# Gate and up products in Strassen's form, and FFNs over two halves of the tokens, in a one-core Hymba layer

## The chip, the core and the metric

The kernel runs on one core of a Trainium2 chip. Five engines work beside each other, each through its own list of instructions in order: TensorE (PE in the profile: matrix products and transposes into PSUM), VectorE (DVE), ScalarE (ACT), GpSimd (POOL) and SyncE (SP, which issues most of the DMAs). The metric is device time in microseconds (us) of one execution.

## The reference

One inference step of a layer over T = 1048 tokens: 16 meta tokens, 1024 of the prompt, 8 samples.

```python
h += 0.5 * swiglu(rmsnorm(h), ffn1_gate, ffn1_up, ffn1_down)
u  = rmsnorm(h) @ w_in              # 1024 -> 4*512 + 512 + 1024 + 8
#    HGRN2 heads (4, dim 128, chunked) and Mamba-2 heads (8, dim 64, chunked scan)
h += concat(hgrn_out, ssm_out) @ w_out
h += 0.5 * swiglu(rmsnorm(h), ffn2_gate, ffn2_up, ffn2_down)
y  = rmsnorm(h)                     # and the final states of both kinds of heads

def swiglu(x, wg, wu, wd):          # wg, wu: 1024 x 2816, wd: 2816 x 1024
    return (silu(x @ wg) * (x @ wu)) @ wd
```

All is float32. The two FFNs hold most of the arithmetic.

## The kernel before

The hidden state h lies feature-major: 8 tiles of 128 features x 1048 tokens. PE multiplies in a format of fewer bits (float32r), so every operand of a product of weights and activations is split into two such parts, x = hi + lo: ACT casts to hi, DVE subtracts hi from x to give lo. `mm3` (L125) makes one product of three matmuls: whi·xhi, whi·xlo, wlo·xhi (L127 to L129). `weights` (L101) reads a block of 128 x 1024 floats by one DMA on SP's queue into one of three `raw` buffers, casts it (L121, ACT) and subtracts (L122, DVE). The tokens are worked in three chunks of 384, 384 and 280 columns (CHUNKS), each in a PSUM bank; there are four banks of the pool `acc` and four of the pool `mis`.

An FFN (`ffn`, L261) goes over the 22 tiles f of 128 hidden features in groups of two. For each f, `gateup` makes x·gate and x·up for the three chunks: 2 x 3 x 8 x 3 = 144 matmuls. ACT takes the SiLU of the gate product (L279), DVE multiplies it with the up product (L283), and ACT and DVE split the result into hi and lo (L285, L286). After each group, `down` multiplies the group before it: 72 matmuls for each f, and 24 evictions by DVE, each adding half a PSUM bank to h (L316). The last `down` takes two groups, chunk by chunk, and calls `after` for every finished tile: `NormAfter` (L197) squares it (ACT, L173), adds the squares up (POOL, L174), sums over the features by a product with a matrix of ones (PE, L184), takes 1/sqrt by Ln and Exp (ACT, with a load of the table that holds both, L154) and makes the operands xhi and xlo of the next product (L190 to L192). Operands of a finished chunk are so made while PE works on the next chunk.

The start (`load_input`, L441) reads nine tiles of 128 tokens, normalizes them token-major, transposes them on PE (L460) into the operands xh and xl, and starts the FFN; after the first gate and up products, `residual` transposes the input a second time (L481) and copies it into h (L483). Between the FFNs come the input projection, the Mamba-2 scan, four HGRN2 heads and the output projection in two halves (`out_proj`, L1028), the second of which ends with `NormAfter` again. After the last `down` of the second FFN, `final` transposes h back, normalizes and writes the output.

No order is written out for the engines: the program issues operations in the order of the Python code, a scheduler gives each engine its list, fixed before the run, and semaphores hold an instruction at the head of its list until its inputs are there and its output buffer is free. What stands behind a waiting instruction on the same engine waits too.

Of the kernel before, what the change touches and what calls it, by code (L numbers as in the profile page):

```python
# [27 lines left out]
CHUNKS = [(0, 384), (384, 384), (768, 280)]  # L28
CW = 384
# [9 lines left out]
class Pack:  # L39
    """small tiles side by side in slots"""  # L40
# [22 lines left out]
class Core:  # L63
    def __init__(self, ctx, tc):
        self.nc = tc.nc
        self.tc = tc
        ent = ctx.enter_context
        self.const = ent(tc.tile_pool(name="const", bufs=1))
        self.wraw = ent(tc.tile_pool(name="wraw", bufs=3))
        self.wsp = ent(tc.tile_pool(name="wsp", bufs=3))  # L70
# [7 lines left out]
        self.finish_norm = None  # L78
# [8 lines left out]

    def t(self, w=CW, tag="t", bufs=7):
        t = self.tmp.tile([P, CW], F32, tag=tag, name=self.uid(tag), bufs=bufs)
        return t[:, :w]  # L90

# [9 lines left out]
    def weights(self, ap, tag=None):  # L101
        """loads [P, nk, nc_] of weights and splits them exactly into two float32r parts"""
        nc_ = ap.shape[-1]
        raw = self.wraw.tile([P, 1024], F32, tag="raw", name=self.uid("raw"))
# [9 lines left out]
        if tag is None:  # L114
            hi = self.wsp.tile([P, 1024], F32R, tag="whi", name=self.uid("whi"))
            lo = self.wsp.tile([P, 1024], F32R, tag="wlo", name=self.uid("wlo"))
        else:
            hi, lo = self.slot(tag, dt=F32R), self.slot(tag, dt=F32R)
        hv = hi[:, : nk * nc_].rearrange("p (k c) -> p k c", k=nk)
        lv = lo[:, : nk * nc_].rearrange("p (k c) -> p k c", k=nk)  # L120
# [4 lines left out]
    def mm3(self, ps, whi, wlo, xhi, xlo, first, last):  # L125
        mm = self.nc.tensor.matmul
        mm(ps, whi, xhi, start=first, stop=False)  # L127
        mm(ps, whi, xlo, start=False, stop=False)  # L128
        mm(ps, wlo, xhi, start=False, stop=last)  # L129
# [12 lines left out]
        # r = A / sqrt(v), then out = r * (3 A^2 - v r^2) with A^3 = 1/2  # L142
# [7 lines left out]
def rstd_wide(K, v, r, after):  # L150
    """r = 1 / sqrt(v), with one Newton step; v is overwritten"""
# [14 lines left out]
def norm_square(K, h, k, c, sq):  # L166
    c0, w = CHUNKS[c]
    nc = K.nc
    hs = h[k][:, c0 : c0 + w]
    if k == 0:  # L170
        return nc.scalar.activation(sq[:, :w], hs, AF.Square)
    t = K.t(w)
    r = nc.scalar.activation(t, hs, AF.Square)  # L173
    nc.gpsimd.tensor_add(sq[:, :w], sq[:, :w], t)  # L174
    return r


def norm_finish(K, h, c, sq, wcol, after):
    """the operands x = rmsnorm(h) * w of chunk c, in two float32r parts"""
    c0, w = CHUNKS[c]  # L180
    cs = slice(c0, c0 + w)
    nc = K.nc
    ps = K.psm()
    nc.tensor.matmul(ps[:, :w], K.ones[D], sq[:, :w], start=True, stop=True)  # L184
    r = K.t(w)
    K.rstd(r, ps[:, :w], w, after)

    def one(k):
        xn = K.t(w)
        nc.vector.scalar_tensor_tensor(xn, h[k][:, cs], wcol[:, k : k + 1], r, ALU.mult, ALU.mult)  # L190
        nc.scalar.copy(K.xhi[k][:, cs], xn)
        (nc.gpsimd if k % 4 == 3 else nc.vector).tensor_sub(K.xlo[k][:, cs], xn, K.xhi[k][:, cs].bitcast(F32))  # L192

    return [lambda k=k: one(k) for k in range(KT)]


class NormAfter:  # L197
    """the norm of h, chunk by chunk as h is finished; the operands of a chunk follow between the steps of the next one"""

    def __init__(self, K, h, wcol, spill=None):  # L200
        self.K, self.h, self.wcol, self.spill = K, h, wcol, spill
        self.sq = new_sq(K)
        self.todo = []

    def __call__(self, k, c):
        K = self.K
        an = norm_square(K, self.h, k, c, self.sq[c])
        if c == 2 and self.spill is not None:
            K.nc.sync.dma_start(self.spill[k * P : (k + 1) * P, :], self.h[k])
        if k == 2 and c > 0:  # L210
            self.finish(c - 1)
        for _ in range(2 if k >= 3 else 0):
            if self.todo:
                self.todo.pop(0)()
        if k == KT - 1:
            self.an = an
            if c == 2:
                K.finish_norm = lambda: self.finish(2)

    def finish(self, c):  # L220
        if c == 0:
            new_x(self.K)
        self.todo += norm_finish(self.K, self.h, c, self.sq[c], self.wcol, self.an)
        if c == 2:
            while self.todo:
                self.todo.pop(0)()


def new_x(K):
    K.xh, K.xl = (K.big.tile([P, KT, T], F32R, tag=n, name=K.uid(n), bufs=1) for n in ("xh", "xl"))  # L230
    K.xhi = [K.xh[:, k] for k in range(KT)]
    K.xlo = [K.xl[:, k] for k in range(KT)]


def new_sq(K):
    return [K.t(tag="sq", bufs=3) for c in range(3)]


def proj(K, wh, wl, evac, chunks=(0, 1, 2)):
    """evac(c0, w, ps) for each chunk of tokens of x @ w"""  # L240
# [8 lines left out]
def proj_first(K, units):  # L249
    """the units after a norm: the last chunk of tokens is ready later than the others"""  # L250
    for c in (0, 1):
        for i, (wh, wl, evac) in enumerate(units):
            proj(K, wh, wl, evac, (c,))
            if K.finish_norm is not None and i == 1:
                K.finish_norm()
                K.finish_norm = None
    for wh, wl, evac in units:
        proj(K, wh, wl, evac, (2,))


def ffn(K, h, wg, wu, wd, after, ready=None, start=None):  # L261
    nc = K.nc
    NG = DFF // 256
    wgv = wg.rearrange("(k p) c -> p k c", p=P)
    wuv = wu.rearrange("(k p) c -> p k c", p=P)
    wdv = wd.rearrange("(g j p) c -> g p j c", p=P, j=2)

    def gateup(g):
        hh, hl = [], []
        for j in range(2):  # L270
            hh.append(K.slot("u", dt=F32R))
            hl.append(K.slot("u", dt=F32R))
        for j in range(2):
            fs = slice((2 * g + j) * P, (2 * g + j + 1) * P)
            ss = {}

            def ev_g(c0, w, ps):
                ss[c0] = K.t(w)
                nc.scalar.activation(ss[c0], ps, AF.Silu)  # L279

            def ev_u(c0, w, ps):
                hd = ss[c0]
                nc.vector.tensor_mul(hd, ps, hd)  # L283
                hiv = hh[j][:, c0 : c0 + w]
                nc.scalar.copy(hiv, hd)  # L285
                nc.vector.tensor_sub(hl[j][:, c0 : c0 + w], hd, hiv.bitcast(F32))  # L286

            if ready is not None and g == 0 and j == 0:
                ws = ready
            else:  # L290
                ws = [K.weights(wgv[:, :, fs]), K.weights(wuv[:, :, fs])]
            units = [(*ws[0], ev_g), (*ws[1], ev_u)]
            if g == 0 and j == 0:
                proj_first(K, units)
                if start is not None:
                    start()
            else:
                for un in units:
                    proj(K, *un)
        return hh, hl  # L300

    def down(gs, hids, chunk_major):
        sp = [[K.weights(wdv[g, :, :, q * 512 : (q + 1) * 512], "u" if len(gs) == 2 and q == 1 else None) for q in range(2)] for g in gs]

        def one(o, c):
            c0, w = CHUNKS[c]
            f = (o % 4) * P
            ps = K.psum()
            n = len(gs) * 2
            for i in range(n):  # L310
                dh, dl = sp[i // 2][o // 4]
                hh, hl = hids[i // 2]
                j = i % 2
                K.mm3(ps[:, :w], dh[:, j, f : f + P], dl[:, j, f : f + P], hh[j][:, c0 : c0 + w], hl[j][:, c0 : c0 + w], i == 0, i == n - 1)
            hs = h[o][:, c0 : c0 + w]
            nc.vector.scalar_tensor_tensor(hs, ps[:, :w], 0.5, hs, ALU.mult, ALU.add)  # L316

        if not chunk_major:
            for o in range(KT):
                for c in range(3):  # L320
                    one(o, c)
        else:
            for c in range(3):
                for o in range(KT):
# [868 lines left out]
```

## Time and profile before

| what | value |
|---|---|
| median of 3 runs | 2220.14 us (2210.18 to 2220.63) |
| the profiled execution: span, and its granted TensorE clock | 2218.1 us, 0.988 |
| busy: PE, DVE, ACT, POOL | 2155.6, 992.8, 597.3, 141.5 us |
| instructions: PE, DVE, ACT | 13770, 1824, 1065 |
| DMA queue of the loads and stores | 127.48 MB, 18.5% of 16 engines |
| first FFN, steady part (66 to 780 us): PE, DVE, ACT busy | 714.0, 255.6, 130.0 us of 714 |
| middle (820 to 1390 us): PE, DVE, ACT busy | 549.5, 336.5, 235.0 us of 570 |
| second FFN, steady part (1450 to 2190 us): PE, DVE, ACT busy | 740.0, 273.1, 133.9 us of 740 |

Busy time is the sum of an engine's instructions, as a share of the span or of a stretch of it. A matmul's recorded time is longer than the distance to the next one, since matmuls are pipelined; the distance between starts is what a matmul costs in a full stream. The profiled execution has no time of its own beside its span; it lies 0.1% under the median.

### The profile page before, as it was taken

What the parts mean: (1) busy time and instruction counts of PE and PEld (TensorE: products, weight loads), DVE (VectorE), ACT (ScalarE), POOL (GpSimd) and SP (SyncE); (2) the same over time, 40 slices, a digit from 0 to 9 for tenths busy, and PEclk for the clock granted to TensorE, in tenths of its full rate; (3) what the DMA queues carried; (4) which work ended last, traced back from release to release, by engine and by line L of the source; (5) the groups of instructions that cost most, each with busy time, mean ns of one, the idle gap of its engine ahead of it and who ended that gap; (6) DMA issues with size and microseconds to landing.
All of it is one profiled execution on the core that took longest, in us unless ns stands there. A gap on an engine that the chain in (4) does not pass through costs nothing.

```text
span 2218.1 us, 32029 instructions
## 1 busy us (share of the span) xinstructions
PE 2155.6 (97%) x13770; PEld 2111.5 (95%) x13770; DVE 992.8 (45%) x1824; ACT 597.3 (27%) x1065; POOL 141.5 (6%) x173
## 2 busy tenths in 40 slices
PE   6999999999999999989999999999999999999998
PEld 5999999999999989968989999999999999999997
DVE  6333334333343376577445466634334343343425
ACT  5311111111111243473522433431111111111112
POOL 1000000000000130231001000400000000000000
PEclk9999999999999999989999999999999999999999
DMA  4111111111111121162212142111111111111112
GB/s 146 48 48 48 44 42 48 48 48 48 40 47 48 58 100 45 55 196 61 82 50 65 55 144 72 29 39 48 48 48 40 47 48 48 48 48 39 48 39 77
DMA packets 173734, 132.19 MB, mean 60 GB/s; under 512 B 8664, under 2 KB 154320, under 8 KB 173584
## 3 DMA queue, kind: packets, MB, share of 16 engines
q1 hardware_dynamic: 172648, 127.48, 18.5%
q10 hardware_dynamic: 720, 2.62, 0.3%
q8 instruction: 108, 1.77, 0.3%
q14 instruction: 34, 0.28, 0.0%
q0 software_dynamic: 224, 0.04, 0.0%
HBM read 114.62 MB, written 15.56 MB: 59 GB/s over the span
## 4 chain that ended last, share of the span: by engine, by line
PE 87%; DVE 5%; issue 3%; DMA 2%; ACT 1%; POOL 1%; SPq 0%; DVEq 0%; POOLq 0%; ACTq 0%
PE acc L128 27%; PE acc L129 27%; PE acc L127 27%; PE mis L923 1%; DVE t L190 1%; DVE xl L192 0%; DMA raw<-in_w_ffn_up_dram 0%; DMA s<-cumd 0%; PE mis L1019 0%; PE mis L481 0%; DMA sst<-sbd 0%; PE mis L962 0%; PE mis L1067 0%; PE mis L980 0%; PE mis L692 0%
## 5 line engine op out<-in xcount | busy, mean ns | idle before, releaser
L127 PE MATMUL acc<-xh,whi 128*128 128x384 f32 (+1 forms) x2880 | 932.7, 324 | 2.2 <-ACT whi L121 1.5
L128 PE MATMUL acc<-xl,whi 128*128 128x384 f32 (+1 forms) x2880 | 933.0, 324 | 0.7 <-DVE xl L464 0.6
L129 PE MATMUL acc<-xh,wlo 128*128 128x384 f32 (+1 forms) x2880 | 931.1, 323 | 0.0
L127 PEld LDWEIGHTS acc<-xh,whi 128*128 128x128 f32 x2880 | 543.0, 189 | 4.2 <-ACT whi L121 1.7
L128 PEld LDWEIGHTS acc<-xl,whi 128*128 128x128 f32 x2880 | 543.4, 189 | 2.6 <-DVE xl L464 1.3
L129 PEld LDWEIGHTS acc<-xh,wlo 128*128 128x128 f32 x2880 | 543.3, 189 | 0.9
L122 DVE TENSOR_TENSOR wlo<-raw,whi 128x1024 fp32r<-128x1024 f32 x162 | 199.3, 1231 | 532.7 <-ACT whi L121 532.0
L121 ACT CAST whi<-raw 128x1024 fp32r<-128x1024 f32 x162 | 169.9, 1049 | 638.1 <-PE acc L128 443.0
L127 PE MATMUL acc<-u,whi 128*128 128x384 f32 (+1 forms) x1008 | 327.6, 325 | 0.0
L128 PE MATMUL acc<-u,whi 128*128 128x384 f32 (+1 forms) x1008 | 326.0, 323 | 0.0
L129 PE MATMUL acc<-u,wlo 128*128 128x384 f32 (+1 forms) x1008 | 325.4, 323 | 0.0
L316 DVE SCALAR_TENSOR_TENSOR s<-acc,s 128x384 f32<-128x384 f32 (+1 forms) x480 | 242.9, 519 | 169.2 <-PE acc L129 167.9
L127 PEld LDWEIGHTS acc<-u,whi 128*128 128x128 f32 x1008 | 190.3, 189 | 0.9 <-issue 0.6
L128 PEld LDWEIGHTS acc<-u,whi 128*128 128x128 f32 x1008 | 190.2, 189 | 0.9 <-issue 0.6
L129 PEld LDWEIGHTS acc<-u,wlo 128*128 128x128 f32 x1008 | 190.2, 189 | 0.0
L283 DVE TENSOR_TENSOR t<-acc,t 128x384 f32<-128x384 f32 x132 | 68.8, 521 | 247.8 <-PE acc L129 245.2
L285 ACT CAST u<-t 128x384 fp32r<-128x384 f32 x132 | 63.7, 483 | 305.1 <-DVE t L283 305.1
L279 ACT ACTIVATE t<-acc 128x384 f32<-128x384 f32 x132 | 60.8, 461 | 281.6 <-PE acc L129 281.5
L174 POOL TENSOR_TENSOR sq<-sq,t 128x384 f32<-128x384 f32 (+1 forms) x42 | 43.3, 1032 | 848.0 <-ACT t L173 796.5
L286 DVE TENSOR_TENSOR u<-t,u 128x384 fp32r<-128x384 f32 x132 | 68.6, 520 | 51.7 <-ACT u L285 51.6
L923 PEld LDWEIGHTS mis<-s,u 128*128 128x128 f32 x320 | 39.0, 197 | 7.9 <-issue 7.8
L129 PE MATMUL acc<-u,u 128*128 128x384 f32 (+1 forms) x144 | 46.4, 322 | 0.0
(326 smaller groups left out, 1454.8 us busy)
## 6 DMA issues: line engine op xcount, KB each, us to landing
raw<-in_w_ffn_gate_dram SPq DMA_DIRECT2D x44, 512.0 KB
raw<-in_w_ffn_up_dram SPq DMA_DIRECT2D x44, 512.0 KB
raw<-in_w_ffn_down_dram SPq DMA_DIRECT2D x44, 512.0 KB
raw<-in_w_in_dram SPq DMA_DIRECT2D x28, 512.0 KB
hspill<-s SPq DMA_DIRECT2D x8, 524.0 KB
s<-hspill SPq DMA_DIRECT2D x8, 524.0 KB
s<-cumd SPq DMA_DIRECT2D x8, 512.0 KB
raw<-in_w_out_dram SPq DMA_DIRECT2D x16, 256.0 KB
```

The costliest lines, as they stand in the source:

```text
L121: self.nc.scalar.copy(hv, src)
L122: self.nc.vector.tensor_sub(lv, src, hv.bitcast(F32))
L127: mm(ps, whi, xhi, start=first, stop=False)
L128: mm(ps, whi, xlo, start=False, stop=False)
L129: mm(ps, wlo, xhi, start=False, stop=last)
L174: nc.gpsimd.tensor_add(sq[:, :w], sq[:, :w], t)
L279: nc.scalar.activation(ss[c0], ps, AF.Silu)
L283: nc.vector.tensor_mul(hd, ps, hd)
L285: nc.scalar.copy(hiv, hd)
L286: nc.vector.tensor_sub(hl[j][:, c0 : c0 + w], hd, hiv.bitcast(F32))
L316: nc.vector.scalar_tensor_tensor(hs, ps[:, :w], 0.5, hs, ALU.mult, ALU.add)
L923: nc.tensor.matmul(ps[:, 64 * c : 64 * c + 64], kg[:, P * c : P * (c + 1)], qv[:, c, :, 1], start=True, stop=True)
```

## The change

Write the gate weights of one tile f over the two halves of the 1024 input features as A11 and A12, the up weights as A21 and A22, and the operand over the same halves, for one half of the tokens (524) split into two quarters of 262, as B11, B12, B21, B22. Gate and up of both quarters are four sums of two block products, eight in all. Strassen's form (in Winograd's variant) makes them of seven block products of sums of blocks, and sums of their results.

In detail:

- `gateup` works one f for one half of the tokens: 7 products of 4 x 3 = 84 matmuls of 262 columns. The weights need four block sums (128 x 512, L289, DVE) and seven splits (128 x 512: cast L294 on ACT, subtraction L295 on DVE). The products go to four PSUM banks a, b, c, d (all of `acc`), three of which are used twice; the sums of results are five additions of 262 columns on DVE (L312, L315, L318, L322, L325), then the SiLUs (L320, L323, ACT), the product (524 columns, L326) and the split of the result (L329, L330).
- `strassen_x` makes the seven operands of one half of the tokens from the normalized h: 8 products with the norm (L229), 8 subtractions (L238), 14 casts (L246) and 14 subtractions of hi (L247), each 128 x 524.
- `ffn` goes over the two halves of the tokens and, in each, over all 22 f, so every gate, up and down weight is read and split twice. `down` takes groups of 2, 4, 4, 4, 4, 4 tiles f; its products are of 262 columns and go to the banks of `mis`; its weights are 4 units of 128 x 1024 for each group and half. After the 22nd f of the first half, `more()` makes the operands of the second half, ahead of the last `down` in the code; after the second half, `between()` makes the first operands of the next stage likewise.
- The norm is the class `Norm`, by quarters of 262 tokens; its 1/sqrt is kept for all tokens (R), and the operands are made from it.
- The input is transposed once: `place` transposes a raw tile into h and makes its norm factor as a row by a product of ones with a diagonal matrix. Five tiles are read and placed first; the other four after the first `gateup` (`later`).
- The second half of the output projection goes over the two halves of the tokens, its weights read and split twice; after the first, `strassen_x` is called for the second FFN. CHUNKS, used by the middle alone, become 350, 350 and 348. The `raw` pool has 4 buffers, and one pool of 6 buffers (`ws`) takes the place of whi and wlo.

```diff
-CHUNKS = [(0, 384), (384, 384), (768, 280)]
+Q = T // 4
+CHUNKS = [(0, 350), (350, 350), (700, 348)]
...
+def strassen_x(K, h, r, wcol, half):
+    nc = K.nc
+    cs = slice(2 * Q * half, 2 * Q * half + 2 * Q)
+    xn = []
+    for kp in range(4):
+        t = K.slot("u", w=4 * Q).rearrange("p (k n) -> p k n", k=2)
+        for j in range(2):
+            k = 2 * kp + j
+            nc.vector.scalar_tensor_tensor(t[:, j], h[k][:, cs], wcol[:, k : k + 1], r[:, cs], ALU.mult, ALU.mult)
+        xn.append(t)
...
+    def operand(x):
+        t = K.xo().rearrange("p s (k n) -> p s k n", k=4)
+        for p in range(2):
+            ks = slice(2 * p, 2 * p + 2)
+            nc.scalar.copy(t[:, 0, ks], x[p])
+            nc.vector.tensor_sub(t[:, 1, ks], x[p], t[:, 0, ks].bitcast(F32))
+        return t
+
+    ops = [operand(b11)]
+    t1 = minus(b12, b11)
+    t2 = minus(b22, t1)
+    ops += [operand(t2), operand(t1), operand(minus(b22, b12)), operand(b21), operand(b22), operand(minus(b21, t2))]
+    return ops
...
+def gateup(K, wg, wu, f, ops):
...
+    def product(ps, x, i, first=True):
+        w = split(x)
+        for k in range(4):
+            hi, lo = w[:, k * P : k * P + P], w[:, 512 + k * P : 512 + k * P + P]
+            K.mm3(ps, hi, lo, ops[i][:, 0, k], ops[i][:, 1, k], first and k == 0, k == 3, not first)
+
+    a, b, c, d = (K.psum()[:, :Q] for i in range(4))
+    product(a, a11, 0)
+    z = K.tq()
+    nc.scalar.copy(z, a)
+    s1 = sum_(a21, a22, ALU.add)
+    s2 = sum_(s1, a11, ALU.subtract)
+    product(b, s2, 1)
+    v = K.tq()
+    nc.vector.tensor_add(v, b, z)
+    product(c, s1, 2)
+    w5 = K.tq()
+    nc.vector.tensor_add(w5, c, v)
+    product(d, sum_(a11, a21, ALU.subtract), 3)
+    gt, ut = (K.t(2 * Q).rearrange("p (n t) -> p n t", n=2) for i in range(2))
+    nc.vector.tensor_add(ut[:, 1], d, w5)
+    product(a, a12, 4, False)
+    nc.scalar.activation(gt[:, 0], a, AF.Silu)
+    product(c, sum_(a12, s2, ALU.subtract), 5, False)
+    nc.vector.tensor_add(gt[:, 1], c, v)
+    nc.scalar.activation(gt[:, 1], gt[:, 1], AF.Silu)
+    product(d, a22, 6, False)
+    nc.vector.tensor_add(ut[:, 0], d, v)
+    nc.vector.tensor_mul(gt, gt, ut)
+    gt = gt.rearrange("p n t -> p (n t)")
+    hid = K.slot("u", w=4 * Q, dt=F32R).rearrange("p (s t) -> p s t", s=2)
+    nc.scalar.copy(hid[:, 0], gt)
+    nc.vector.tensor_sub(hid[:, 1], gt, hid[:, 0].bitcast(F32))
+    return hid
...
+    for half in range(2):
+        hids, f0, due = [], 0, []
+        for f in range(NF):
+            hids.append(gateup(K, wgv, wuv, f, ops))
+            if half == 0 and f == 0 and start is not None:
+                start()
+            if due:
+                down(half, *due.pop(), False)
+            if f % 4 == 1 and f < NF - 1:
+                due.append((f0, hids))
+                hids, f0 = [], f + 1
+        if half == 0:
+            ops = more()
+        else:
+            between()
+        down(half, f0, hids, True)
...
+    for i in range(5):
+        read(i)
+    parameters(K, a)
+    for i in range(5):
+        place(i)
+
+    def later():
+        for i in range(5, 9):
+            read(i)
+            place(i)
...
-    out_proj(K, a, h, 1, opb, NormAfter(K, h, K.pc["norm_ffn2"]))
+    def after2(k, q):
+        nf2.add(k, q)
+        if k == KT - 1 and q == 1:
+            ops.extend(strassen_x(K, h, nf2.r, wn2, 0))
```

More of the change, by code (lines that the diff above doesn't have):

```diff
@@ L113, in weights, with split @@
         src = raw[:, : nk * nc_].rearrange("p (k c) -> p k c", k=nk)
[L114 to L120, printed above, removed]
+        return self.split(src, self.ws(), self.ws())
+    def split(self, src, hi, lo):
+        n, k, c = src.shape
+        hv = hi[:, : k * c].rearrange("p (k c) -> p k c", k=k)
+        lv = lo[:, : k * c].rearrange("p (k c) -> p k c", k=k)
         self.nc.scalar.copy(hv, src)
@@ L197 @@
[L197 to L226, printed above, removed]
@@ L229, in new_x, with __init__, add @@
[L229 to L236, printed above, removed]
+class Norm:
+    def __init__(self, K, h):
+        self.K, self.h = K, h
+        self.r = K.big.tile([P, T], F32, tag="R", name=K.uid("R"), bufs=1)
+        self.sq = {}
+    def add(self, k, q):
+        K = self.K
+        hs = self.h[k][:, q * Q : q * Q + Q]
+        if k == 0:
+            self.sq[q] = K.t(Q)
+            an = K.nc.scalar.activation(self.sq[q], hs, AF.Square)
+        else:
+            t = K.t(Q)
+            an = K.nc.scalar.activation(t, hs, AF.Square)
+            K.nc.gpsimd.tensor_add(self.sq[q], self.sq[q], t)
+        if k == KT - 1:
+            ps = K.psm()
+            K.nc.tensor.matmul(ps[:, :Q], K.ones[D], self.sq[q], start=True, stop=True)
+            K.rstd(self.r[:, q * Q : q * Q + Q], ps[:, :Q], Q, an)
@@ L249, in proj_first, with sum_, split @@
 def proj_first(K, units):
-    for c in (0, 1):
-        for i, (wh, wl, evac) in enumerate(units):
+    for c in range(3):
+        for wh, wl, evac in units:
             proj(K, wh, wl, evac, (c,))
[L254 to L261, printed above, removed]
-    nc = K.nc
-    NG = DFF // 256
+def gateup(K, wg, wu, f, ops):
+    nc = K.nc
+    fs = slice(f * P, f * P + P)
+    raws = []
+    for w in (wg, wu):
+        t = K.raw()
+        nc.sync.dma_start(t.rearrange("p (k c) -> p k c", k=KT), w[:, :, fs])
+        raws.append(t)
+    a11, a12 = raws[0][:, 0:512], raws[0][:, 512:1024]
+    a21, a22 = raws[1][:, 0:512], raws[1][:, 512:1024]
+    def sum_(x, y, op):
+        t = K.t(512)
+        nc.vector.tensor_tensor(t, x, y, op)
+        return t
+    def split(x):
+        t = K.ws()
+        nc.scalar.copy(t[:, 0:512], x)
+        nc.vector.tensor_sub(t[:, 512:1024], x, t[:, 0:512].bitcast(F32))
+        return t
+    def product(ps, x, i, first=True):
[31 more added lines that the diff above has]
+    return hid
@@ L264, in ffn @@
+def ffn(K, h, wg, wu, wd, ops, more, between, after, start=None):
+    nc = K.nc
+    NF = DFF // P
     wgv = wg.rearrange("(k p) c -> p k c", p=P)
     wuv = wu.rearrange("(k p) c -> p k c", p=P)
[L266 to L321, printed above, removed]
-        else:
-            for c in range(3):
-                for o in range(KT):
-                    one(o, c)
-                    after(o, c)
@@ L328, in ffn, with down, unit, one @@
-    prev = None
-    for g in range(NG):
-        cur = gateup(g)
-        if g == NG - 1:
-            down([g - 1, g], [prev, cur], True)
-        elif prev is not None:
-            down([g - 1], [prev], False)
-        prev = cur
+    wdv = wd.rearrange("(f p) c -> p f c", p=P)
+    def down(half, f0, hids, last):
+        n = len(hids)
+        def unit(q, tag=None):
+            raw = K.raw()[:, : n * 256].rearrange("p (f c) -> p f c", f=n)
+            nc.sync.dma_start(raw, wdv[:, f0 : f0 + n, q * 256 : q * 256 + 256])
+            parts = [K.slot(tag, dt=F32R) if tag else K.ws() for i in range(2)]
+            return K.split(raw, *parts)
+        def one(un, o, c):
+            ps = K.psm()[:, :Q]
+            fs = slice((o % 2) * P, (o % 2) * P + P)
+            for i, hid in enumerate(hids):
+                K.mm3(ps, un[0][:, i, fs], un[1][:, i, fs], hid[:, 0, c * Q : c * Q + Q], hid[:, 1, c * Q : c * Q + Q], i == 0, i == n - 1)
+            q = 2 * half + c
+            hs = h[o][:, q * Q : q * Q + Q]
+            nc.vector.scalar_tensor_tensor(hs, ps, 0.5, hs, ALU.mult, ALU.add)
+            if last:
+                after(o, q)
+        if last and half == 1:
+            units = [unit(q, "u" if q >= 2 else None) for q in range(4)]
+            for c in range(2):
+                for o in range(KT):
+                    one(units[o // 2], o, c)
+        else:
+            for q in range(4):
+                un = unit(q)
+                for o in (2 * q, 2 * q + 1):
+                    for c in range(2):
+                        one(un, o, c)
@@ L753, in sample @@
     def sample(b):
-        s = K.wraw.tile([P, 1024], F32, tag="raw", name=K.uid("sst"))
+        s = K.raw("sst")
         sb = s[:, 0:512].rearrange("p (j n) -> p j n", j=4)
@@ L989, in samples @@
     def samples(b0):
-        s = K.wraw.tile([P, 1024], F32, tag="raw", name=K.uid("hst"))
+        s = K.raw("hst")
         sb = s[:, 0:512].rearrange("p (b v) -> p b v", b=4)
```

202 lines of the change are left out of this document (106 added, 96 removed).

## The prediction

> **What bounds the kernel now.** I read the page first (busy shares, the chain that ended last), then busy times by stretch, then the starts of matmuls in a full stream, the DVE groups by shape, and last the idle times of PE at the seams.
>
> ```profile
> span 2218.1 us, 32029 instructions
> ...
> PE 2155.6 (97%) x13770; PEld 2111.5 (95%) x13770; DVE 992.8 (45%) x1824; ACT 597.3 (27%) x1065; POOL 141.5 (6%) x173
> ...
> PE 87%; DVE 5%; issue 3%; DMA 2%; ACT 1%; POOL 1%; SPq 0%; DVEq 0%; POOLq 0%; ACTq 0%
> ```
> PE is the bound: 97% busy, 87% of the chain.
>
> ```profile
> 0.00:25.00 25.00, 5.08 (x24) 3.98 (x24) 11.40 (x34) 13.92 (x25) 10.16 (x34) 1.00 0.83 277
> 25.00:66.00 41.00, 39.79 (x264) 37.37 (x265) 31.09 (x92) 24.88 (x62) 0.00 (x0) 0.96 0.19 55
> 66.00:780.00 714.00, 714.00 (x4462) 713.23 (x4462) 255.58 (x427) 129.97 (x214) 8.09 (x8) 1.00 0.15 46
> 780.00:820.00 40.00, 35.59 (x220) 34.07 (x219) 30.50 (x49) 22.07 (x41) 18.16 (x20) 0.96 0.39 137
> ```
> Columns: stretch, then busy us of PE, PE's weight loads, DVE, ACT, POOL, granted clock, DMA share, GB/s. Inside the first FFN PE never stops and DVE works 36% of the time; PE's idle lies at the start and at the seams.
>
> ```profile
> 303.63 0.33 PE L129 MATMUL acc<-xh,wlo 128*128 128x384 f32 x1
> 303.80 0.29 PE L127 MATMUL acc<-xh,whi 128*128 128x280 f32 x1
> 303.93 0.29 PE L128 MATMUL acc<-xl,whi 128*128 128x280 f32 x1
> 304.06 0.29 PE L129 MATMUL acc<-xh,wlo 128*128 128x280 f32 x1
> ...
> 816.80 0.34 PE L129 MATMUL acc<-xh,wlo 128*128 128x384 f32 x1
> 818.23 0.74 PE L184 MATMUL mis<-sq,ones 128*128 128x280 f32 x2 [1.09 <-POOL sq L174]
> ```
> First column: start. A matmul costs the distance between starts: from 299.78 to 303.80 the 23 of 384 columns take 174.8 ns each, the 24 of 280 to 306.89 take 128.8. So time goes by columns (0.46 ns each). After the 1.4 us gap at 816.8 the stream goes on at full rate.
>
> ```profile
> L122 DVE TENSOR_TENSOR wlo<-raw,whi 128x1024 fp32r<-128x1024 f32 x162 | 199.3, 1231 | 532.7 <-ACT whi L121 532.0
> L316 DVE SCALAR_TENSOR_TENSOR s<-acc,s 128x384 f32<-128x384 f32 x320 | 174.7, 555 | 138.0 <-PE acc L129 136.7
> L286 DVE TENSOR_TENSOR u<-t,u 128x384 fp32r<-128x384 f32 x88 | 49.1, 558 | 51.2 <-ACT u L285 51.1
> ...
> L464 DVE TENSOR_TENSOR xl<-mis,xh 128x512 fp32r<-128x512 f32 x16 | 10.2, 682 | 1.5 <-ACT xh L463 1.5
> ```
> ```profile
> 31.73 1.29 DVE L464 TENSOR_TENSOR xl<-mis,xh 128x512 fp32r<-128x512 f32 x2 [0.83 <-ACT xh L463]
> ```
> DVE prices by width (mean ns behind the bar). Two of 512 back to back take 1.29 us, so one fills 0.61 and ends 0.68 after its start. By width I estimate 0.34 (0.42 to its end) for 262 columns, 0.62 for 524, 0.65 for 524 with the norm (half of the 1284 ns of L456), 1.14 for 1024 (1231 less the same 0.08).
>
> **The change, part by part.** The sum is against the profiled 2218.1 us, 0.1% under the median.
>
> *PE's columns.* Gate and up of one f: 48 matmuls on each chunk, 48 x (2 x 0.1748 + 0.1288) = 22.96 us. After: 2 x 84 = 168 of 262 columns. At 0.46 ns a column 0.1205 each, 20.24 us. Times 44: -120. Down: 24 x (2 x 0.1748 + 0.1288) = 11.48 to 96 x 0.1205 = 11.57 us, times 44: +4. Net **-116**. The 262-wide step isn't in the trace: its ends are 0.112 (the 16 transposes of L481 take 1.75 us, 0.109 each, so a weight load fits under that) and 0.1288 (no shorter than 280), -99 and +96 on 11,616 matmuls; I take 0.1205, as 262 is 6% from 280.
>
> *A new wait in each gateup.* The static order of after puts on DVE's queue, behind product d's end: the sum into ut (L318), the sum a12 - s2 for product 5 (L289), then two sums for the *next* f, and only then the subtraction of product 5 (L295). From the end of product d: 0.2 (hand-over, as L283 starts after L129) + 0.42 + 0.60 + 0.60 + 0.68 + 0.68 = 3.2 us until product 5 has its lo. PE has meanwhile product 4 (12 matmuls, 1.45) and the six of product 5 that need hi alone (0.72): 2.17. So PE stands about 1.0 us in 64 of 88 gateups; in the 24 ahead of a down no next sums stand there and ACT's cast ends last, about 0.8. **+84** (35 to 130: four DVE steps at 0.45, or at 0.75). Behind that subtraction the next f's splits queue, but those have 3 us of PE work as cover. DVE's whole need is 11 x 0.61 + 5 x 0.34 + 2 x 0.62 = 9.7 us for 10.12 us of PE: no slack to catch up. ACT's need (7 casts of 0.60 from L463's 588 ns, 4 smaller: about 6 us) hides under PE.
>
> *Loads.* FFN weights are read twice, about +70 MB on 127: the queue's 18.5% becomes about 29%. A pair of raw tiles has a gateup's 11 us to land where one takes 4.5: hidden, 0; without cover it would be 4.5 us a gateup.
>
> *Start.* Now the first real matmul starts at 25.1, the first f ends at 57.0 (22.96 us of it work) and the second transposes (L481) take 7.9: 42 us beside the work. After: 5 tiles are copied into h by DVE and ACT in turn till about 32 us; then on DVE 8 norm products (to 36), and 23 further operations ahead of product 1's lo, so product 0 starts near 37, product 1 near 51, the first gateup ends near 64. Then PE's list has the transposes of tiles 5 to 8 behind product 0 of the second gateup, and tile 5's load is on ACT's queue behind the first gateup's last cast: it lands near 71, and each tile has its chain of square (1.06 us), table load (1.28), 1/sqrt. The second gateup goes on near 88 to 94 with 11.6 us of work done: 65 to 82 beside the work. **+35** (+10 if SP and ACT issue the loads at once, +45).
>
> *Middle of FFN 1.* `more()` puts 28 to 30 operations of `strassen_x` (8 x 0.65 + 22 x 0.62 = 19 us) on DVE ahead of the down's first eviction (L359). PE has four banks of `mis`, 4 x 1.45 = 5.8 us after about 2 us of waiting for the hid; it stands about 12 to 15. At the next half's first gateup the Exp of `Norm` stands ahead of the casts on ACT: 7 to 8. With 2 for the clock **+23** (12 to 30).
>
> *FFN 1 to the middle.* `between()`: 16 operands and 4 unit splits, about 15 us of DVE, ahead of the first eviction: stands 10.5 where now 4.4 + 1.5 are lost: **+5** (-3 to +10).
>
> *Output projection to FFN 2.* Now 4.5 + 2.5 are lost. After: `strassen_x` (28 operations) ahead of an eviction while four `acc` banks hold 5.8 us: 13, and 8 for the norm at the end, 2 for the clock: **+16** (5 to 25).
>
> *Middle of FFN 2.* As in FFN 1, 15, and the `final` of tiles 0 to 3 on PE ahead of the next product 0, 5: **+20** (8 to 28).
>
> *Clock.* After the 3.3 us idle at 794 the 280-wide matmuls run at 0.233 from 798.7 to 801: half rate, 1.7 us lost. With four new long gaps **+6**. Chunks of 350 have the same columns: 0.
>
> Sum: -116 + 84 + 35 + 23 + 5 + 16 + 20 + 6 = +73: about **2290 us** (+3%).
>
> **Rivals.**
> 1. *DVE's queue is not on the path* (faster). Then the 84 and the DVE blocks (15 + 15 + 13 + 5 at the seams) are hidden: -132, **2158**. For it: DVE is 45% busy and waits now on PE or ACT in nearly every group. Against it: the order is fixed, the sums for the next f stand ahead. At half of that cost the time is 2224 (*same*, between 2207 and 2229); faster by over 0.5% from under 0.37 of it.
> 2. *DVE sets the pace of each gateup*: its operations wait for one another, so each costs its whole duration: 11 x 0.68 + 5 x 0.42 + 2 x 0.70 = 11.0 and the 0.8 of waiting for PE, 11.9 in place of 11.1 in 64 gateups: +50, **2340**. For it: no slack. Against: back-to-back pairs overlap (1.29 for two).
> 3. *The clock falls at every stall*: 1.7 us lost in each of 88 gateups, +150, **2440**. Against it: the 1.4 us gap at 816.8 left the rate alone. [...]
>
> **How the numbers follow.** Forecast 2255 to 2325: 0.52. Rival 2: 0.17. Rival 3: 0.04. Same: 0.09. Rival 1: 0.18. A change of 0.5% (11 us) is about what runs of this kernel can tell from none. Slower 0.73, same 0.09, faster 0.18. The range leaves out most of rival 1, rival 3 and the upper edge of 2: 2190 to 2345.
>
> **What would show it.** PE starts of 262 columns every 0.1205 us. One idle time of about 1 us on PE in each gateup, ahead of product 5, put down to DVE ws L295; PE share near 90%, DVE above 75%. PE idle of over 10 us three times, ahead of L359's evictions, and product 1 of the first gateup near 51 us. Wrong it is if DVE shows idle time ended by PE all through the gateups, or if the 262-wide step is not in proportion to its columns.

## The result

The changed kernel takes 2398.84 us (median of 4, 2396.52 to 2404.74) against 2216.57 us for the kernel before (4 runs): 1.0828 times as long, 95% interval 1.0798 to 1.0857. The forecast was 2290 us, slower, with a range from 2190 to 2345: the direction was right, the size was less than half of what came. The profiled execution took 2404.74 us, its span is 2403.0, so 185 us have to be found against the 2218.1 of before.

The page of the changed kernel, in the order in which the page of before was read (span, busy shares, the costliest PE, DVE and ACT groups of the gate and up products):

```profile
span 2403.0 us, 39323 instructions
...
PE 2147.0 (89%) x15928; PEld 2051.3 (85%) x15928; DVE 1646.1 (68%) x3121; ACT 933.6 (39%) x1782; POOL 133.7 (6%) x175
...
L140 PE MATMUL acc<-xo,ws 128*128 128x262 f32 (+2 forms) x3232 | 989.6, 306 | 122.1 <-ACT ws L294 68.9
...
L295 DVE TENSOR_TENSOR ws<-t,ws 128x512 fp32r<-128x512 f32 x352 | 239.9, 687 | 71.3 <-ACT ws L294 67.4
...
L294 ACT CAST ws<-t 128x512 fp32r<-128x512 f32 x352 | 208.0, 617 | 102.4 <-PE mis L141 79.7
```

PE's share fell from 97% to 89%; it stands idle for 256 us in place of 62. The prices of the operations are those of the prediction (a subtraction of 512 columns 0.687 us, a cast 0.617). DVE works 68% of the time, and it, too, has long idle times: it is not the bound by its sum.

Busy times by stretch (stretch, busy us of PE, its weight loads, DVE, ACT, POOL, granted clock, DMA share, GB/s): the start, the first half of FFN 1, its middle, its second half, the seam to the middle of the kernel, then the seam to FFN 2 and the middle of FFN 2:

```profile
0.00:88.20 88.20, 38.02 (x188) 34.04 (x188) 52.01 (x168) 38.99 (x96) 10.13 (x34) 0.73 0.28 86
88.20:445.50 357.30, 336.10 (x2615) 323.76 (x2616) 261.70 (x474) 133.74 (x252) 0.00 (x0) 0.99 0.30 88
445.50:495.40 49.90, 28.90 (x212) 27.61 (x210) 34.97 (x61) 22.77 (x44) 11.12 (x14) 0.79 0.18 51
495.40:863.90 368.50, 346.17 (x2699) 333.41 (x2700) 273.11 (x498) 138.33 (x264) 0.30 (x3) 1.00 0.30 88
863.90:910.60 46.70, 33.15 (x230) 31.28 (x229) 35.15 (x70) 24.45 (x48) 12.59 (x14) 0.83 0.56 175
...
1486.00:1558.40 72.40, 52.88 (x406) 51.24 (x404) 47.05 (x84) 36.94 (x68) 24.84 (x28) 0.90 0.15 44
...
1928.00:1983.80 55.80, 30.99 (x228) 29.75 (x226) 39.84 (x89) 17.82 (x40) 0.00 (x0) 0.78 0.16 54
```

Two kinds of loss show. PE is idle for 50 us at the start and for 14 to 25 at each of the four seams, where the clock is lower as well (0.73 to 0.90). And it is idle for 21 to 22 us in each half of an FFN, where before it never stopped.

What happens in the steady part is the same in each gateup. PE's matmuls around product 5 (first column: start):

```profile
298.52 0.28 PE L142 MATMUL acc<-xo,ws 128*128 128x262 f32 x1
299.79 0.39 PE L140 MATMUL acc<-xo,ws 128*128 128x262 f32 x1 [0.99 <-DVE t L289]
300.02 0.29 PE L141 MATMUL acc<-xo,ws 128*128 128x262 f32 x1
300.31 0.39 PE L140 MATMUL acc<-xo,ws 128*128 128x262 f32 x1
300.53 0.28 PE L141 MATMUL acc<-xo,ws 128*128 128x262 f32 x1
300.83 0.39 PE L140 MATMUL acc<-xo,ws 128*128 128x262 f32 x1
301.06 0.28 PE L141 MATMUL acc<-xo,ws 128*128 128x262 f32 x1
301.18 0.28 PE L142 MATMUL acc<-xo,ws 128*128 128x262 f32 x1
301.30 0.28 PE L140 MATMUL acc<-xo,ws 128*128 128x262 f32 x1
```

and ACT and DVE in the same time:

```profile
298.84 0.39 ACT L320 ACTIVATE t<-acc 128x262 f32<-128x262 f32 x1 [3.91 <-PE acc L142]
299.13 0.61 ACT L294 CAST ws<-t 128x512 fp32r<-128x512 f32 x1
...
299.63 1.14 ACT L294 CAST ws<-raw 128x512 fp32r<-128x512 f32 x2
```
```profile
297.38 0.43 DVE L318 TENSOR_TENSOR t<-acc,tq 128x262 f32<-128x262 f32 x1 [0.88 <-PE acc L142]
297.73 0.68 DVE L289 TENSOR_TENSOR t<-raw,t 128x512 f32<-128x512 f32 x1
298.33 0.68 DVE L289 TENSOR_TENSOR t<-raw 128x512 f32<-128x512 f32 x1
299.05 0.69 DVE L289 TENSOR_TENSOR t<-t,raw 128x512 f32<-128x512 f32 x1
299.77 0.69 DVE L295 TENSOR_TENSOR ws<-t,ws 128x512 fp32r<-128x512 f32 x1
```

From 298.52 to 299.79 PE starts nothing: 1.27 us in place of 0.12. Then six matmuls come in pairs, 0.52 us from pair to pair, in place of 0.24. Only from 301.18 does the stream run at 0.12 us a matmul again. Four gateups without a down, from 124.63 to the next down's first matmul at 172.54, take 47.91 us for 336 matmuls: 11.98 us each. Without stops the trace has 0.1219 us from matmul to matmul (mean of the steps under 0.14 us from 95 to 440 us), and 84 x 0.1219 would be 10.24. So about 1.74 us are lost in each of 88 gateups, 153 us, and the forecast had 84.

The DVE list is as it was read from the static order: the subtraction for product 5 (299.77) ends 3.1 us behind product 3. But ACT had the SiLU of the gate's first quarter (L320, started 298.84, when product 4 was done) ahead of the cast for product 5, whose input was ready at 298.41; the cast started at 299.13, 0.72 us later. And the six matmuls are not all of product 5: PE's list has one pair each for product 5, product 6 and the next f's product 0, and each pair waits for its own cast.

### The profile page after: what moved, and what is told of

The parts are those of the page before. It is cut to its first block, busy times and chain, and to the rows that moved or that the text cites. A ratio compares the mean times of both kernels' runs of the same rounds, so it can differ in the third digit from the quotient of the medians.

```text
span 2403.0 us, 39323 instructions
## 1 busy us (share of the span) xinstructions
PE 2147.0 (89%) x15928; PEld 2051.3 (85%) x15928; DVE 1646.1 (68%) x3121; ACT 933.6 (39%) x1782; POOL 133.7 (6%) x175
## 3 DMA queue, kind: packets, MB, share of 16 engines
q1 hardware_dynamic: 300968, 198.79, 28.1%
## 4 chain that ended last, share of the span: by engine, by line
PE 46%; DVE 6%; ACT 1%; issue 1%; DMA 0%; POOL 0%; POOLq 0%; DVEq 0%; ACTq 0%
PE acc L140 11%; PE acc L142 9%; PE acc L141 9%; PE mis L140 3%; PE mis L141 3%; PE mis L142 3%; DVE t L289 2%; PE mis L961 1%; DVE xo L247 1%; ACT ws L294 0%; PE mis L1057 0%; DVE u L229 0%; PE mis L1000 0%; DVE t L238 0%; DVE y L1113 0%
## 5 line engine op out<-in xcount | busy, mean ns | idle before, releaser
L140 PE MATMUL acc<-xo,ws 128*128 128x262 f32 (+2 forms) x3232 | 989.6, 306 | 122.1 <-ACT ws L294 68.9
L141 PE MATMUL acc<-xo,ws 128*128 128x262 f32 (+2 forms) x3232 | 960.9, 297 | 5.7 <-DVE xo L247 3.6
L142 PE MATMUL acc<-xo,ws 128*128 128x262 f32 (+2 forms) x3232 | 935.0, 297 | 0.7 <-DVE ws L295 0.7
L140 PEld LDWEIGHTS acc<-xo,ws 128*128 128x128 f32 x3232 | 620.0, 192 | 176.5 <-ACT ws L294 167.9
L141 PEld LDWEIGHTS acc<-xo,ws 128*128 128x128 f32 x3232 | 621.8, 192 | 7.0 <-DVE xo L247 3.9
L142 PEld LDWEIGHTS acc<-xo,ws 128*128 128x128 f32 x3232 | 608.2, 191 | 2.3 <-DVE ws L295 1.8
L140 PE MATMUL mis<-u,ws 128*128 128x262 f32 x1344 | 385.0, 287 | 45.8 <-DVE s L359 31.5
L142 PE MATMUL mis<-u,ws 128*128 128x262 f32 x1344 | 385.0, 287 | 0.6 <-DVE ws L134 0.6
L141 PE MATMUL mis<-u,ws 128*128 128x262 f32 x1344 | 384.4, 286 | 0.0
L140 PEld LDWEIGHTS mis<-u,ws 128*128 128x128 f32 x1344 | 257.5, 192 | 46.7 <-DVE s L359 31.9
L295 DVE TENSOR_TENSOR ws<-t,ws 128x512 fp32r<-128x512 f32 x352 | 239.9, 687 | 71.3 <-ACT ws L294 67.4
L142 PEld LDWEIGHTS mis<-u,ws 128*128 128x128 f32 x1344 | 256.8, 191 | 0.9 <-DVE ws L134 0.9
L359 DVE SCALAR_TENSOR_TENSOR s<-mis,s 128x262 f32<-128x262 f32 x384 | 157.2, 426 | 145.2 <-PE mis L142 144.2
L141 PEld LDWEIGHTS mis<-u,ws 128*128 128x128 f32 x1344 | 256.2, 191 | 0.1
L294 ACT CAST ws<-t 128x512 fp32r<-128x512 f32 x352 | 208.0, 617 | 102.4 <-PE mis L141 79.7
L294 ACT CAST ws<-raw 128x512 fp32r<-128x512 f32 x264 | 157.5, 621 | 164.6 <-PE mis L141 161.4
L134 DVE TENSOR_TENSOR ws<-raw,ws 128x1024 fp32r<-128x1024 f32 (+1 forms) x132 | 153.1, 1163 | 89.9 <-ACT ws L133 89.8
L320 ACT ACTIVATE t<-acc 128x262 f32<-128x262 f32 x88 | 34.3, 390 | 377.2 <-PE acc L142 377.2
L295 DVE TENSOR_TENSOR ws<-raw,ws 128x512 fp32r<-128x512 f32 x264 | 175.7, 685 | 3.9
L318 DVE TENSOR_TENSOR t<-acc,tq 128x262 f32<-128x262 f32 x88 | 37.9, 430 | 81.2 <-PE acc L142 81.2
L196 POOL TENSOR_TENSOR t<-t,t 128x262 f32<-128x262 f32 x56 | 48.5, 873 | 631.1 <-ACT t L195 574.5
```

Source lines behind the costliest of these rows:

```text
L134: self.nc.vector.tensor_sub(lv, src, hv.bitcast(F32))
L140: mm(ps, whi, xhi, start=first, stop=False, skip_group_check=more)
L141: mm(ps, whi, xlo, start=False, stop=False, skip_group_check=more)
L142: mm(ps, wlo, xhi, start=False, stop=last, skip_group_check=more)
L196: K.nc.gpsimd.tensor_add(self.sq[q], self.sq[q], t)
L294: nc.scalar.copy(t[:, 0:512], x)
```

## The experiments

Theory A: ACT's list holds PE; the SiLU, which has to wait for product 4, stands ahead of three casts. Theory B, the one of the prediction: DVE's list holds PE, by the sums for the next f ahead of the subtraction for product 5. The profile alone doesn't decide. The waits of PE in the changed kernel:

```profile
PE acc L140 <- ACT ws L294: 68.9, 48, 12.0
PE acc L140 <- DVE t L289: 45.3, 46, 1.0
PE mis L140 <- DVE s L359: 31.9, 3, 15.7
PE acc L140 <- DVE s L1079: 13.7, 1, 13.7
```

The same stop of 1 us is put down to ACT in about half of the gateups and to DVE in the other half: in the rows above the cast for product 5 (299.13 + 0.61) and DVE's second sum for the next f (299.05 + 0.69) end at the same 299.74, and of the two it is the cast's output (ws) that the matmul reads.

**The SiLU's wait taken away.**

```diff
     product(a, a12, 4, False)
-    nc.scalar.activation(gt[:, 0], a, AF.Silu)
+    nc.scalar.activation(gt[:, 0], z, AF.Silu)
```

The gate's first quarter so lacks the sum with product 4.

> The first SiLU of each gateup (L320) reads z, the copy of product 0 that ACT made long before, in place of bank a after product 4. It so leaves the sum with product 4 out of the gate's first quarter; the lists of PE, DVE and ACT keep their order, and only the wait of L320 for product 4 is gone. Theory A (ACT's list holds PE: L320 waits for the end of product 4 and stands ahead of the casts for product 5, product 6 and the next product 0): the casts start about 0.5 us earlier, the subtraction on DVE, 3.2 us behind product 3, is then last, and each gateup is shorter by 0.5 to 0.6 us: 88 x 0.55 = 48 us, about 2350. Theory B (the prediction's: DVE's list alone, with the sums for the next f ahead of that subtraction): no change, 2395 to 2405.

Measured: 2338.89 us (2333.88 to 2343.59), 1.0543 times the kernel before (1.0524 to 1.0562): 60 us less than the changed kernel. PE around product 5, and ACT:

```profile
288.15 0.28 PE L142 MATMUL acc<-xo,ws 128*128 128x262 f32 x1
288.74 0.39 PE L140 MATMUL acc<-xo,ws 128*128 128x262 f32 x1 [0.31 <-ACT ws L294]
288.96 0.28 PE L141 MATMUL acc<-xo,ws 128*128 128x262 f32 x1
289.26 0.39 PE L140 MATMUL acc<-xo,ws 128*128 128x262 f32 x1
```
```profile
288.06 0.62 ACT L294 CAST ws<-t 128x512 fp32r<-128x512 f32 x1 [3.18 <-DVE t L289]
288.59 1.14 ACT L294 CAST ws<-raw 128x512 fp32r<-128x512 f32 x2
```

The cast now starts as soon as its sum is made, and the gap ahead of product 5 is 0.59 us in place of 1.27. The lists of DVE and ACT keep the order of the changed kernel, DVE's next sums ahead of the subtraction included, and PE's differs by one pair of matmuls in four gateups. Theory A holds, and 0.68 us of each gateup's 1.74 are the SiLU's. The pairs still come 0.52 us apart, and they still follow the casts (0.53 us apart). I had expected DVE's subtraction to end last then; it doesn't, the waits that were divided between ACT and DVE are now all put down to casts:

```profile
PE acc L140 <- ACT ws L294: 53.6, 94, 12.0
```

**DVE's list alone mended.** The next f's first sum is put behind the subtraction for product 5 (`K.sub5`; the first gateup has none before it).

```diff
-    s1 = sum_(a21, a22, ALU.add)
+    if K.sub5 is not None:
+        with K.tc.issue_after(K.sub5.ins):
+            s1 = sum_(a21, a22, ALU.add)
+    else:
+        s1 = sum_(a21, a22, ALU.add)
...
     product(c, sum_(a12, s2, ALU.subtract), 5, False)
+    K.sub5 = K.sub
```

> The sums for the next f are put behind the subtraction for product 5 on DVE's list; ACT's list keeps the SiLU ahead of the casts. Theory B (prediction): the stop shrinks by 1.0 us in 64 gateups, about 2340. Theory A: the cast of product 5 still comes behind the SiLU, so nothing is gained: 2390 to 2410.

Measured: 2410.39 us (2408.86 to 2414.73), 1.087 (1.0852 to 1.0889): nothing gained, about 10 us lost. PE's waits for casts, and the subtraction for product 5 on DVE (L296 in this kernel; L295 is the cast):

```profile
PE acc L141 <- ACT ws L295: 114.4, 95, 12.0
```
```profile
298.47 0.68 DVE L290 TENSOR_TENSOR t<-raw,t 128x512 f32<-128x512 f32 x1
300.51 0.69 DVE L296 TENSOR_TENSOR ws<-t,ws 128x512 fp32r<-128x512 f32 x1 [1.36 <-ACT ws L295]
```

The next sums no longer stand between the sum and the subtraction, but DVE now waits 1.36 us there for the cast. Ahead of product 5 the gap is 1.26 us as before, and all of the 114 us that were divided between ACT and DVE (68.9 and 45.3) are put down to casts. A second place, where matmuls come 0.22 to 0.29 us apart in place of 0.12, has come up ahead of the stop. Theory B falls: what the prediction named as the cause was there, but it was not what ended last.

**The sum made early.** One line moved, to where its inputs are ready.

```diff
     s2 = sum_(s1, a11, ALU.subtract)
+    s4 = sum_(a12, s2, ALU.subtract)
     product(b, s2, 1)
...
-    product(c, sum_(a12, s2, ALU.subtract), 5, False)
+    product(c, s4, 5, False)
```

> One line moved: the sum a12 - s2 for product 5, which needs only weights, is made right behind s2 and not behind the addition of product 3's result. Its cast and subtraction can then stand ahead of the SiLU (ACT) and of the additions (DVE). Both theories A and B: the stop ahead of product 5 goes, and nothing else waits in a gateup; 88 x 1.82 = 160 us less, about 2243, if no other wait takes its place. If DVE is the bound of a gateup by its sum (rival 2 of the prediction), the gateup stays at 11 us or more and the time above 2320.

Measured: 2246.44 us (2241.55 to 2253.18), 1.0129 (1.0107 to 1.0151): 152 us less, from one line. The waits of PE, and busy times over 42 us of gateups and down:

```profile
PE mis L140 <- DVE s L360: 30.1, 2, 15.0
PE acc L140 <- ACT ws L294: 26.2, 6, 12.0
PE acc L140 <- DVE s L1080: 13.7, 1, 13.7
```
```profile
118.00:160.00 42.00, 42.00 (x348) 42.00 (x347) 38.48 (x68) 22.92 (x44) 0.00 (x0) 1.00 0.42 122
```

The waits in the gateups fell from 94 (48 and 46) to 6, and PE is busy for the whole 42 us, with DVE busy for 38.5 of them. So DVE, at 92%, is close to being the bound of a gateup, but is not (rival 2). With the sum early, cast and subtraction for product 5 and 6 stand ahead of the SiLU and of the addition of product 3's result, and none of them waits for PE. The sum's place behind product 3 was so the root of the stop: it sent the cast behind the SiLU.

**The seams alone.** On the changed kernel, with its stops in the gateups:

```diff
-        if half == 0:
-            ops = more()
-        else:
+        if half == 1:
             between()
         down(half, f0, hids, True)
+        if half == 0:
+            ops = more()
...
-        if k == KT - 1 and q == 1:
-            ops.extend(strassen_x(K, h, nf2.r, wn2, 0))
     out_proj(K, a, h, 1, opb, after2)
+    ops.extend(strassen_x(K, h, nf2.r, wn2, 0))
```

> At the seams alone: the last down of the first half is issued ahead of the operands of the second half, and the operands of FFN 2 behind the whole second half of the output projection, so that DVE's list has evictions between the operand steps. If the operands ahead of the evictions hold PE at the seams (16.0 us in the middle of FFN 1, 16.0 in FFN 2, 14.0 at the output projection in the trace): 12 to 15 us less at each, 35 to 45 in all, about 2362. Rival: the operands come later in turn and the next half's first product waits for them instead: no change or up to 10 us less.

Measured: 2378.83 us (2372.89 to 2382.37), 1.0721 (1.0701 to 1.074): 20 us less, half of what was expected. The stops ahead of the evictions (16.0, 14.0, 16.0 us in the starts of matmuls) are gone. In the middle of FFN 2 the gain stays; in the middle of FFN 1 and at the output projection the next half's first product now starts 16.2 and 16.3 us late in place of 3.5 and 3.4. The rival is true for two seams of three: the stop moved. The list of DVE there shows why: from 463 to 472 us, with evictions a microsecond apart, none of the operand's subtractions (L238) comes in between. I took it that their output buffers, of the pool t, were still held by squares that POOL had to add; that isn't shown by itself, since the next run changes it together with two other things.

**Sum, seams, and differences in place.** The differences of the operands are written over the blocks that they are made from, so that they need no buffer of the pool t; the order of the operand steps changes with it.

```diff
+    s4 = sum_(a12, s2, ALU.subtract)
...
-    t1 = minus(b12, b11)
-    t2 = minus(b22, t1)
...
+    t1 = minus(b12, b11, b11)
+    o5 = operand(b22)
+    o2 = operand(t1)
+    d = minus(b22, b12, b12)
+    t2 = minus(b22, t1, b22)
...
+        if half == 0:
+            ops = more()
...
+    ops.extend(strassen_x(K, h, nf2.r, wn2, 0))
```

> Together: the sum a12 - s2 early; the down ahead of the next operands and FFN 2's operands behind the output projection; and the differences in strassen_x written over the blocks that they come from, in place of tiles of the pool t, whose buffers the squares of the norm hold at the seams. Against 2246 of the early sum alone: a seam has about 32 us of DVE work (30 operand steps, 16 evictions, 4 splits, the norm) and the first gateup 10 more, against 23 + 10 us of PE work, so 8 to 12 us of stop should be left of 22 to 25 at each of three seams: about 2210. If the order at the seams is not the cause, or the norm's chain holds the first product of the next half anyway, 2235 to 2246.

Measured: 2206.8 us (median of 8, 2202.4 to 2210.04), 0.9967 (0.9955 to 0.9979): as expected, and a little faster than the kernel before. In the middle of FFN 1 PE's waits are now down to these, for the norm's squares and for the first casts of the next half:

```profile
PE mis L199 <- POOL t L196: 6.4, 2, 5.3
PE acc L140 <- ACT ws L297: 5.9, 1, 5.9
```

**Without Strassen.** The changed kernel, with eight block products in place of seven, and no sums:

```diff
-    product(a, a11, 0)
...
+    for x, y, up in ((a11, a12, False), (a21, a22, True)):
+        w0, w1 = split(x), split(y)
+        for n in range(2):
+            ps = K.psum()[:, :Q]
+            product(ps, w0, n, True)
+            product(ps, w1, 2 + n, False)
+            if up:
+                nc.vector.tensor_mul(gt[:, n], ps, gt[:, n])
+            else:
+                nc.scalar.activation(gt[:, n], ps, AF.Silu)
```

> The kernel after with the Strassen form taken out and the rest kept: halves of the tokens, 262 columns, all weights read and split twice; gate and up as eight block products (96 matmuls for each f and half), four splits, no sums. If the loss is made by Strassen's extra steps in each gateup, a gateup takes 96 x 0.1206 = 11.6 us with no stop, against 11.95 with Strassen: 88 x 0.37 = 32 us less, and the operands of a half need 16 steps of DVE in place of 30, some 8 us less at each of three seams and at the start: about 2340, so that Strassen as made costs more than its matmuls save. Rival: halving alone (narrow matmuls, weights split twice on ACT and DVE) is what costs: then the time stays at 2400 or above.

Measured: 2293.61 us (2281.95 to 2295.36), 1.0347 (1.0319 to 1.0375). Its page:

```profile
PE 2183.6 (96%) x16984; PEld 2141.8 (94%) x16984; DVE 1092.8 (48%) x2097; ACT 770.5 (34%) x1406; POOL 137.3 (6%) x175
```

Four gateups take 46.61 us (from 93.18 to 139.79): 11.65 each, as expected. So a gateup of the changed kernel (11.98) is longer than one without Strassen, and one with the sum early (four in 40.86 us, from 116.07 to 156.93, 10.21 each) is 1.44 us shorter. The rest went further than I had expected, to 2294 and not 2340: the three seams stop PE for 7.2, 7.0 and 7.2 us where the changed kernel has 16.0, 14.0 and 16.0, and by 54.4 us 172 gate and up matmuls are done, where the changed kernel has done 96 by 63.8. Strassen as made costs about 4.6% of the time (1.0828 against 1.0347); with one line moved it gains about 2% (1.0129 against 1.0347). The rest of the change, with the halves and the weights split twice, costs the 3.5% that this kernel has over the one before; how that divides among its parts isn't shown.

**The start.** On top of the kernel with the mended seams, all nine tiles are read at once, and the last four are placed ahead of the first gateup in the code:

```diff
-    for i in range(5):
+    for i in range(9):
         read(i)
...
     ops = strassen_x(K, h, r1, wn1, 0)
+    for i in range(5, 9):
+        place(i)
```

> The same as the kernel with the mended seams, and at the start all nine tiles are read at once and tiles 5 to 8 are transposed ahead of the first gateup's end, while PE waits for product 1; squares go to one spare buffer. In the trace of after PE does 5 us of work between 63.8 and 88.2, where it waits for the loads and norm factors of tiles 5 to 8; 15 to 20 us less than the kernel with the mended seams: about 2193. If the operand steps on DVE set the start alone, 0 to 5 us less.

Measured: 2199.11 us (2194.44 to 2199.7), 0.9927 (0.9912 to 0.9942): 8 us less than the kernel with the mended seams, where 15 to 20 were expected. The stop between 64 and 88 us is gone, but one has come ahead of product 1: PE's list has the new transposes there, and they wait for a norm factor that stands behind the operand steps on DVE:

```profile
PE mis L519 <- DVE t L517: 15.9, 2, 10.9
```

**Norm factors first.** The factors of tiles 5 to 8 are made ahead of the operand steps, the transposes stay behind the first gateup:

```diff
-    ops = strassen_x(K, h, r1, wn1, 0)
-    for i in range(5, 9):
-        place(i)
+    for i in range(5, 9):
+        factor(i)
+    ops = strassen_x(K, h, r1, wn1, 0)
```

> As the kernel with all tiles read at the start, but only the norm factors of tiles 5 to 8 are made ahead of the operand steps on DVE; their transposes and copies come after the first gateup. In the trace of the kernel before it PE waits 11 us at 40.2 for such a factor (DVE, L517), which stands behind the operand steps, and product 1 starts at 58.7 in place of 46.6. If that is so, product 1 starts near 49 and the time is 4 to 8 us less: about 2193. If the copies only move behind the first gateup and delay the second there, no change: 2197 to 2201.

Measured: 2193.25 us (2187.93 to 2195.07), 0.9891 (0.987 to 0.9913). Product 1 starts at 48.5 us, the time is 6 us less, as expected, and this is the fastest of all: 1.1% less than the kernel before.

## Why the prediction was right and wrong

| step of the sum | predicted | measured |
|---|---|---|
| PE's columns | -116 | 7392 + 4224 matmuls at 0.1219 (1416), against 44 x 216 at 0.1600 (714 us for 4462 in the profile of before; 1521): -105 |
| a new wait in each gateup | +84 | 88 x 1.74 = +153 |
| start | +35 | 88.2 less 11.6 of work, less one gateup's stop (1.8), less the 42 of before, is 33; with 2 lost at half clock behind 88.2 (granted 0.50 from 88.2 to 92.5): +35 |
| middle of FFN 1 | +23 | +27 |
| FFN 1 to the middle | +5 | about +11 |
| output projection to FFN 2 | +16 | about +17 |
| middle of FFN 2 | +20 | about +34 |
| clock | +6 | in the rows above |
| sum | +73 | about 172 of the 185 |

The seams' measured numbers are the time from the last gate and up matmul ahead of a seam to the first behind it (in the middle of FFN 1 to product 1, with product 0 counted as work), less 0.122 us for each 262-wide matmul (and the transposes), with 1.7 us for each spell at half clock behind it (as in the kernel before from 798.7 to 801 us, granted clock 0.50), less the same for the kernel before. Of the 13 us that are left, about 5 lie at the end of FFN 2, where PE stands from 2372.0 to 2376.2 us for `final` (DVE, L1113) and matmuls at first start 0.22 us apart or more behind that; for the others I have no place.

The step that failed is "a new wait in each gateup", with the sentence "ACT's need ... hides under PE". The place was right, and so was the time at which DVE has product 5's lo (3.2 us behind product 3, in the trace 3.1). What was wrong is what PE and ACT do until then. I took six matmuls of product 5 that need hi alone as cover, with their hi there. In the list they are two each of products 5, 6 and the next 0, and each pair needs a cast of its own; and the first of these casts stands behind a SiLU that waits for product 4. I summed ACT's work (6 us of 10), and did not walk through ACT's list as I did through DVE's. The run with the SiLU's wait gone shows this part (0.68 us of the 1.74); the run with DVE's list mended shows that DVE's part, the one forecast, was worth nothing while ACT's stood; and the early sum removes both. The sign that the prediction named, idle time of PE put down to DVE's ws of L295, came to 0.7 us in the whole execution, and DVE was busy for 68%, not for over 75%:

```profile
PE acc L142 <- DVE ws L295: 0.7, 4, 0.2
```

That the gap ahead of product 5 (1.27 us) came near the forecast of 1.0 was luck, since another engine ended it. By the forecast the columns and the new wait together made the kernel 32 us faster, and only the seams made it slower; measured, those two alone make it 48 us slower. All other gateups lose the same: the 24 ahead of a down have the gap of 1.27 us too, not 0.8 in all.

The second miss is the middle of FFN 2: PE stands 15.7 us for the eviction as forecast (15), but also 4.2 us between the transposes of `final` (for the output tiles of L1113) and 5.2 ahead of the next half's first product, where I had put 5 in all, and it then starts a matmul every 0.22 us in place of 0.12 from 1984.8 to 1986.8 and from 1990.5 to 1994.0 us (granted clock 0.50 and 0.53).

Right, or nearly, were the matmul's step (0.1219 us for 262 columns, 0.1205 forecast, which is most of the 11 us that the row of PE's columns came short), the loads (28.1% of the queue, 29% forecast, and PE waits for none in the gateups), the start as a whole (product 0 from 28 to 34.8 and product 1 at 47, earlier than forecast, the first gateup and product 0 of the second over at 63.8, the second going on at 88.2; forecast 37, 51, 64, 88 to 94), and the stops ahead of L359 (15.7 us).

On the rivals: rival 1 was wrong for this kernel: at the seams DVE's list holds PE (15.7 us ahead of L359), and in the gateups the cast that PE waits for stands behind a late sum on DVE. But the 84 of its 132 us that lay in the gateups could all be hidden with DVE's work unchanged, as the early sum shows. Rival 2, DVE as the bound, would have come to 2340, nearer than the forecast, but for the wrong reason: with the stops gone DVE is 92% busy and PE never waits in the 42 us of gateups and down (118 to 160). Rival 3, the clock, is refuted: with a stop of 1.3 us in every gateup of 12 the granted clock is 0.99 from 88.2 to 445.5, and 1.00 from 92.5 on. It is low at the start and in the middles of the two FFNs (0.73, 0.79, 0.78), where PE's longest stops are 12.0, 15.7 and 15.7 us.

## What to carry to other kernels

When the bound engine is to get less work, walk through the lists of all engines that feed it, not only of the busiest: an engine at 39% held PE, because one instruction that waits stood ahead of three that had their inputs. Trace an operation that needs only weights where its inputs are ready, not where its result is used: one line moved was worth 152 us. And where a mended stop turns up again at the next product, look at what the moved work needs next: a buffer (as I took it here, which isn't shown by itself), or another engine's list, as at the start.

## What was not expected of the hardware

The stop of a gateup is the same to a hundredth of a microsecond in nearly all 88 gateups (1.26 or 1.27 us between starts), while the profile puts it down to ACT in half of them and to DVE in the other half; the run that changed ACT's wait alone shortened it everywhere (0.58 to 0.62 us), and the run that moved DVE's sums left it as it was. And over the first 88.2 us of the changed kernel, where PE's work comes in pieces between stops of up to 12.0 us, the granted clock is 0.73; in the kernel before it was 1.00 to 25 us and 0.96 from there to 66.
